# Feed-forward output projections as seven block products in place of direct ones

## The chip, the cores and the metric

The kernel runs on one core of a Trainium2 chip. The metric is the device time of one launch in microseconds; lower is better. The core has five engines with a queue each: TensorE (PE) multiplies matrices, VectorE (DVE), ScalarE (ACT) and GpSimd (POOL) work on elements, and SyncE (SP) issues most DMA transfers. Every queue is worked off strictly in its own order; engines wait for each other by semaphores.

## The reference

One decoder layer on 1024 prompt tokens and 8 single-token samples, 1032 columns in all (kept transposed: channels on partitions, tokens along the free dimension). The part that matters:

```python
D_MODEL, D_FF = 1024, 2816
def _swiglu(h, wi, wo):
    u = h @ wi                            # 1024 -> 2 * 2816
    gate, up = u[..., :D_FF], u[..., D_FF:]
    return (jax.nn.silu(gate) * up) @ wo  # 2816 -> 1024

h = _layer_norm(DN_ALPHA * h + 0.5 * _swiglu(h, ffn1_wi, ffn1_wo), g0, b0)
mix, ... = _mixer(h, ...)                 # RWKV-7 and RG-LRU branches
h = _layer_norm(DN_ALPHA * h + mix, g1, b1)
h = _layer_norm(DN_ALPHA * h + _xattn(h, ...), g2, b2)
h = _layer_norm(DN_ALPHA * h + 0.5 * _swiglu(h, ffn2_wi, ffn2_wo), g3, b3)
```

## The kernel before

Every fp32 operand of a matrix product is split into a high and a low part (ACT copies the high part, DVE subtracts: `split`, L228 and L229), and each product is three matmuls into the same psum tile (`mm3`, L125 to L127). `raw_tile` gives the staging tile into which a DMA loads what is to be split.

The function `ffn` runs twice, first (FFN1) and last (FFN2) in the program. `KT` is 8 tiles of 128 input channels, `JT` is 22 tiles of 128 hidden channels, `HN` is 258, a quarter of the 1032 columns.

The **up stage** computes hidden tiles 0 and 1 directly (`classic`) and the other 20 in ten pairs (`pair(j)`, j = 2, 4, ... 20). A pair has two halves, gate and up; a half multiplies a 2x2 block of weight by a 2x2 block of activations in seven block products instead of eight ("forms", in the order B11, B21, T1, B22, T2, T3, T4), each for two column halves p. So the stage has 20 half-pairs; the text calls them h0 to h19. `left(j)` loads four weight blocks of 128x512 per half-pair and makes four weight sums of them on POOL (L334, through `pool_tt`); the fourth of these sums is split for the form B22. DVE puts the products together into the hidden tiles `g` (`TT`, L333), and SP stores them to DRAM (`HID`, L407).

The **down stage** multiplies the 22 hidden tiles by `wo` directly: they are taken in eight groups of two or three; `loads` brings a group's tiles back from `HID`, loads its rows of `wo` and splits both; for each of 8 output tiles and 3 column chunks of 344 (`CH3`), `down_tile` sums a group in psum and DVE adds it to the accumulator `acc` (L442). POOL adds the residual `src` (L464). The last group is woven with the layer norm of the three chunks (`ln_stat_step`, `ln_finish`).

The order in which each queue gets its instructions is set by a scheduler from the program's dependencies and buffers, not by the order of the source lines.

Of the kernel before, what the change touches and what calls it, by code (L numbers as in the profile page):

```python
# [153 lines left out]
def ln_finish(S, st, li, c0, n, final=None, keep=None):  # L154

    S.pend.append((c0, c0 + n))
    return ln_stream(S, st, li, c0, n, final, keep)


def ln_stream(S, st, li, c0, n, final, keep):  # L160
# [11 lines left out]
    adds = nc.gpsimd if final is None or c0 + n < NT else nc.vector  # L172
# [49 lines left out]
LN_STEPS = 20  # L222

# [59 lines left out]
def ffn(S, octx, wi, wo, li, src, pre=(), final=None, keep=None, after=None):  # L283
# [5 lines left out]

    nc, tc = S.nc, S.tc  # L290
    HID = S.dram.tile([JT, 128, NT], F32, name="HID%d" % li)
    with ExitStack() as ctx:
# [39 lines left out]
        gt = pool(uctx, "fg", 6)  # L332
        TT = lambda o, a, b, op: nc.vector.tensor_tensor(out=o, in0=a, in1=b, op=op)  # L333
# [30 lines left out]
        def pair(j):  # L364
# [46 lines left out]
        groups = [[0, 1]] + [[3 * g + i for i in (2, 3, 4)] for g in range(5)] + [[17, 18], [19, 20, 21]]  # L411
        hd, wt = {}, {}
        S.hlseq = itertools.cycle([S.whl] * 2 + [S.hlx] * 2)

        def loads(js, to=None):
            for j in js:
                hd[j] = to() if to else (S.HH[:, j % KT, :], S.HL[:, j % KT, :])
                for p in range(2):
                    N = slice(2 * HN * p, 2 * HN * p + 2 * HN)
                    x = raw_tile(S)  # L420
                    nc.sync.dma_start(out=x, in_=HID[j, :, N])
                    split(nc, [t[:, N] for t in hd[j]], x)
                wt[j] = load_split(S, wo[128 * j:128 * j + 128, :])

        loads(groups[0])
        uctx.close()
        S.norms = Norms(S, octx, 344)
        hlast = pool(ctx, "fhl", 3)
        xw = pool(ctx, "fwo", 5)
        S.hlseq = itertools.cycle([S.hlx] * 2 + [xw] * 2 + [S.whl] * 3 + [xw] * 3 + [S.hlx] * 2)  # L430

        def down_tile(js, m, ni, st=None):
            c0, n = CH3[ni]
            q = psum(n)
# [11 lines left out]
        def down_last(js, ni, st):
            for m in range(KT):
                down_tile(js, m, ni, st)
                yield

        banks = itertools.cycle([ps])
        last = lambda: [hlast.tile([128, NT], F32R, tag="h" + x, name="h" + x) for x in "hl"]
        for g, js in enumerate(groups[:-1]):
            loads(groups[g + 1], last if g + 2 == len(groups) else None)
            for m in range(KT):
                for ni in range(3):
                    down_tile(js, m, ni)
            if 2 <= g < 6:
                for k in (2 * g - 4, 2 * g - 3):
                    for p in range(2):  # L460
                        a = S.acc[:, k, 2 * HN * p:2 * HN * p + 2 * HN]
                        x = raw_tile(S)
                        nc.sync.dma_start(out=x, in_=src[k, :, 2 * HN * p:2 * HN * p + 2 * HN])
                        nc.gpsimd.tensor_tensor(out=a, in0=a, in1=x, op=ALU.add)  # L464
        if after is not None:
            ahead(S, after)
        pre = []
        for ni in range(3):
            st = SimpleNamespace()
            weave((down_last(groups[-1], ni, st), KT), *pre)  # L470
            pre = [(ln_finish(S, st, li, *CH3[ni], final, keep), LN_STEPS)]
# [72 lines left out]
def mixer(octx, S, I, O, MG, HD, pre):  # L544
# [13 lines left out]
    with ExitStack() as ctx:  # L558
# [807 lines left out]
        return [norm(3)]  # L1366
# [49 lines left out]
def attention(S, I, li, pre, after, keep):  # L1416
# [3 lines left out]
    with ExitStack() as ctx:  # L1420
# [200 lines left out]
        return [norm(3)]  # L1621
# [121 lines left out]
```

## Time and profile before

| | us |
|---|---|
| median of three runs | 3177.53 |
| fastest, slowest of them | 3172.7, 3178.56 |
| profiled execution, its own time | 3173.59 |
| its span (first to last instruction) | 3171.8 |
| PE busy in the span | 2997.5 (95%) |
| DVE busy | 2196.4 (69%) |
| ACT busy | 1433.0 (45%) |
| POOL busy | 669.7 (21%) |
| down stage of FFN1, 459.7 to 726.4 | 266.7 |
| down stage of FFN2, 2884.5 to 3145.1 | 260.6 |

The profiled execution is 3.9 us faster than the median. Busy shares are over the whole span; the work below is done by stage, since the stages have different limits.

### The profile page before, as it was taken

The page shows a single profiled execution, that of the slowest core. Times are in us where ns is not written, and L with a number is a line of the kernel's source. Part 1 is how long each engine was busy: PE and PEld are TensorE (multiplying, and loading weights), DVE is VectorE, ACT ScalarE, POOL GpSimd, SP SyncE. Part 2 cuts the span into 40 slices and gives each one's busy share as a digit, 9 for nine tenths or more (in the row PEclk, how much of TensorE's full clock was granted, in tenths as well). Part 3 has the DMA queues.
Part 4 walks back from the last instruction along what each step waited for, and adds up shares of the span by engine and source line. Part 5 has one row for each costly group of instructions (what it writes and reads, how often), then busy time and mean ns, then how long its engine had stood idle before and what let it go on. Part 6 is the DMA issues. An engine that isn't in the chain of part 4 may idle for free. (4 is left out here: it accounts for less than half of the span.)

```text
span 3171.8 us, 63384 instructions
## 1 busy us (share of the span) xinstructions
PE 2997.5 (95%) x23324; PEld 2835.5 (89%) x23324; DVE 2196.4 (69%) x5903; ACT 1433.0 (45%) x3193; POOL 669.7 (21%) x718
## 2 busy tenths in 40 slices
PE   8999999999999999999999989889897999999997
PEld 8999999998888888888887768788897999999997
DVE  7666665564367788877787877666778666666556
ACT  5333342125465565566556655354235333334212
POOL 2222210123021121122112122350005222220111
PEclk9999999999999999999999979799998999999998
DMA  4222243413645555545554454654433222225321
GB/s 139 79 83 78 81 148 109 126 49 110 223 134 137 142 146 145 143 133 144 147 147 131 140 161 131 183 168 134 147 121 121 73 78 81 78 80 161 111 84 54
DMA packets 375943, 386.74 MB, mean 122 GB/s; under 512 B 153904, under 2 KB 267600, under 8 KB 375632
## 3 DMA queue, kind: packets, MB, share of 16 engines
q1 hardware_dynamic: 363344, 348.86, 37.3%
q0 software_dynamic: 12288, 33.83, 3.0%
q8 instruction: 183, 3.00, 0.4%
q14 instruction: 128, 1.05, 0.1%
HBM read 277.54 MB, written 105.23 MB: 121 GB/s over the span
## 5 line engine op out<-in xcount | busy, mean ns | idle before, releaser
L125 PE MATMUL ps<-HH,wh 128*128 128x258 f32 (+1 forms) x2384 | 718.7, 302 | 18.3 <-ACT HH L510 7.4
L126 PE MATMUL ps<-HL,wh 128*128 128x258 f32 (+1 forms) x2384 | 717.1, 301 | 0.6 <-POOL HL L215 0.6
L127 PE MATMUL ps<-HH,wl 128*128 128x258 f32 (+1 forms) x2384 | 715.9, 300 | 0.0
L125 PE MATMUL g<-HH,wh 128*128 128x344 f32 (+2 forms) x1840 | 618.5, 337 | 20.7 <-ACT ev L556 4.5
L127 PE MATMUL g<-HH,wl 128*128 128x344 f32 (+2 forms) x1840 | 596.1, 325 | 2.2 <-DVE wl L100 2.2
L126 PE MATMUL g<-HL,wh 128*128 128x344 f32 (+2 forms) x1840 | 594.1, 323 | 0.5 <-POOL HL L215 0.2
L125 PEld LDWEIGHTS ps<-HH,wh 128*128 128x128 f32 x2384 | 451.4, 189 | 20.7 <-ACT HH L510 7.4
L126 PEld LDWEIGHTS ps<-HL,wh 128*128 128x128 f32 x2384 | 451.2, 189 | 1.4 <-POOL HL L215 0.9
L127 PEld LDWEIGHTS ps<-HH,wl 128*128 128x128 f32 x2384 | 450.6, 189 | 0.0
L125 PEld LDWEIGHTS g<-HH,wh 128*128 128x128 f32 x1840 | 354.5, 193 | 38.1 <-ACT ev L556 6.3
L127 PEld LDWEIGHTS g<-HH,wl 128*128 128x128 f32 x1840 | 354.0, 193 | 7.4 <-DVE wl L100 3.1
L126 PEld LDWEIGHTS g<-HL,wh 128*128 128x128 f32 x1840 | 355.2, 193 | 5.5 <-POOL HL L215 1.4
L334 POOL TENSOR_TENSOR raw<-raw 128x512 f32<-128x512 f32 x160 | 213.8, 1336 | 566.0 <-DVE wl L229 359.0
L228 ACT ACTIVATE wh<-raw 128x512 fp32r<-128x512 f32 x280 | 176.5, 631 | 322.0 <-PE ps L126 260.9
L229 DVE TENSOR_TENSOR wl<-raw,wh 128x512 fp32r<-128x512 f32 x280 | 203.0, 726 | 139.0 <-ACT wh L228 132.1
L99 ACT ACTIVATE wh<-raw 128x512 fp32r<-128x512 f32 x302 | 185.1, 626 | 221.8 <-PE ps L126 77.6
L100 DVE TENSOR_TENSOR wl<-raw,wh 128x512 fp32r<-128x512 f32 x302 | 217.7, 728 | 91.8 <-ACT wh L99 89.4
L442 DVE SCALAR_TENSOR_TENSOR acc<-ps,acc 128x344 f32<-128x344 f32 x336 | 168.4, 512 | 144.2 <-PE ps L127 143.5
L644 POOL DMA_DIRECT2D GD<-ev x150 | 84.4, 563 | 632.5 <-ACT ev L556 411.8
L551 DVE TENSOR_TENSOR pr<-tq,iv 128x2 f32<-128x2 f32 (+30 forms) x496 | 159.7, 322 | 2.8
L556 ACT ACTIVATE ev<-g 128x344 f32<-128x344 f32 x192 | 86.9, 453 | 106.1 <-PE g L127 103.6
L464 POOL TENSOR_TENSOR acc<-acc,raw 128x516 f32<-128x516 f32 x32 | 42.7, 1340 | 420.0 <-DVE acc L442 322.4
(407 smaller groups left out, 6515.5 us busy)
## 6 DMA issues: line engine op xcount, KB each, us to landing
raw<-in_wi_dram SPq DMA_DIRECT2D x176, 256.0 KB
raw<-in_w_in_dram SPq DMA_DIRECT2D x116, 256.0 KB
raw<-in_wo_dram SPq DMA_DIRECT2D x104, 256.0 KB
GD<-ev POOLq DMA_DIRECT2D x150, 172.0 KB, 2.6
raw<-HID SPq DMA_DIRECT2D x88, 258.0 KB
HID<-g SPq DMA_DIRECT2D x80, 258.0 KB
tg<-GD SPq DMA_DIRECT2D x32, 512.0 KB
wt<-T SPq DMA_DIRECT2D x160, 64.0 KB
```

What stands on the lines that cost most here:

```text
L99: nc.scalar.activation(out=hi, in_=raw, func=AF.Identity)
L100: S.low.tensor_tensor(out=lo, in0=raw, in1=hi.bitcast(F32), op=ALU.subtract)
L125: nc.tensor.matmul(ps, wh, xh, start=first, stop=False)
L126: nc.tensor.matmul(ps, wh, xl, start=False, stop=False)
L127: nc.tensor.matmul(ps, wl, xh, start=False, stop=last)
L228: nc.scalar.activation(out=hi, in_=x, func=AF.Identity)
L229: nc.vector.tensor_tensor(out=lo, in0=x, in1=hi.bitcast(F32), op=ALU.subtract)
L334: pool_tt = lambda o, a, b, op: nc.gpsimd.tensor_tensor(out=o, in0=a, in1=b, op=op)
L442: nc.vector.scalar_tensor_tensor(out=a, in0=q, scalar=0.5 / ALPHA, in1=a, op0=ALU.mult, op1=ALU.add)
L551: TTo = lambda o, a, b, op: nc.vector.tensor_tensor(out=o, in0=a, in1=b, op=op)
L556: ACT = lambda o, a, f=AF.Identity, **kw: nc.scalar.activation(out=o, in_=a, func=f, **kw)
L644: (nc.gpsimd if then else nc.sync).dma_start(out=GD[p][:, gi, c0:c0 + n], in_=e)
```

## The change

It is all in `ffn` and the layer norm that follows it.

- **Up stage, `hidden(i, G)`:** after each pair POOL makes four differences of the hidden blocks (T1 to T4, in eight instructions of 128x258) and issues ten stores from its own queue into `HF`, one array per form. The four stores of SP into `HID` go away.
- **Up stage, `sums(i)`:** for each pair SP loads four blocks of `wo` (128x512) into the tiles w0 to w3, POOL makes four sums of 128x512 and issues four stores of them into `WF`. The pool `ff` has one buffer of each of these tiles. `hidden(0)` and `sums(0)` are for hidden tiles 0 and 1.
- **Down stage:** seven forms times two column halves make 14 passes. A pass sums one form over all 11 pairs of hidden tiles in four psum tiles of 258 columns (132 matmuls), then adds the four results to one or two quarters of `acc`. During the first pass of a form, the next form's activations are loaded from `HF` and split (`hid_prep`), during the second its weights (`w_prep`). The residual `src` is loaded straight into `acc`.
- **Layer norm:** four chunks of 258 columns instead of three of 344, beginning at the passes of T3 and T4, with two buffers for the running sum and a number of empty steps before a chunk's second part (`lag`); where a norm is woven with other work its step count is multiplied by four (`first_of`, also for the norms that the mixer and the attention hand on).

```diff
-            for m in range(2):
-                for p in range(2):
-                    nc.sync.dma_start(out=HID[j + m, :, 2 * HN * p:2 * HN * p + 2 * HN], in_=G[m][p])
+            hidden(j // 2, G)
+
+        def hidden(i, G):
+            T = [ft.tile([128, 2 * HN], F32, tag="t%d" % t, name="t%d" % t) for t in range(4)]
+            sub = lambda o, a, b: pool_tt(o, a, b, ALU.subtract)
+            for p in range(2):
+                (b11, b12), (b21, b22) = ((g[p][:, :HN], g[p][:, HN:]) for g in G)
+                N = slice(HN * p, HN * p + HN)
+                t1, t2, t3, t4 = (t[:, N] for t in T)
+                for f, b in ((0, b11), (1, b21), (3, b22)):
+                    nc.gpsimd.dma_start(out=HF[i, f, :, N], in_=b)
+                sub(t1, b12, b11)
+                sub(t3, b22, b12)
+                sub(t2, b22, t1)
+                sub(t4, t2, b21)
+            for f, t in zip((2, 4, 5, 6), T):
+                nc.gpsimd.dma_start(out=HF[i, f], in_=t)
+
+        def sums(i):
+            t = [ft.tile([128, 512], F32, tag="w%d" % x, name="w%d" % x) for x in range(5)]
+            for x, b in zip(t, ((0, 0), (0, 1), (1, 1), (1, 0))):
+                nc.sync.dma_start(out=x, in_=weight(i, *b))
+            yield
+            a11, a21, a22, a12, s1 = t
+            pool_tt(s1, a21, a22, ALU.add)
+            pool_tt(a21, a11, a21, ALU.subtract)
+            pool_tt(a11, a22, a21, ALU.subtract)
+            pool_tt(a12, a12, a11, ALU.subtract)
+            for n, x in enumerate((s1, a11, a21, a12)):
+                nc.gpsimd.dma_start(out=WF[i, n], in_=x)
+            yield
 
         for j in range(2, JT, 2):
+            w = sums(j // 2)
+            next(w)
             pair(j)
...
+        def one_pass(f, p, st=None):
...
+            qs = [psum(HN) for _ in range(4)]
+            for k in range(NJ):
+                if f < 6:
+                    (w_prep if p else hid_prep)(f + 1, k)
+                for m in range(4):
+                    step(m, k, qs[m])
+                yield
+            for m in range(4):
+                result(m, qs[m])
...
+        for k in range(KT):
+            nc.sync.dma_start(out=S.acc[:, k, :], in_=src[k])
+        pre = []
+        for f, p in itertools.product(range(7), range(2)):
+            st = SimpleNamespace() if f > 4 else None
+            weave((one_pass(f, p, st), NJ), *pre)
...
```

What the scheduler makes of it shows in the queues. First POOL's queue in the up stage of FFN1, where `raw` are weight blocks of the up stage. Before, a half-pair's four sums follow each other and nothing lies between them; these two groups of four are those of h4 and h5:

```order
L334 TENSOR_TENSOR raw_1760<-raw_1756,raw_1758 128x512
L334 TENSOR_TENSOR raw_1756<-raw_1752,raw_1756 128x512
L334 TENSOR_TENSOR raw_1752<-raw_1760,raw_1752 128x512
L334 TENSOR_TENSOR raw_1754<-raw_1754,raw_1752 128x512
L334 TENSOR_TENSOR raw_2019<-raw_2015,raw_2017 128x512
L334 TENSOR_TENSOR raw_2015<-raw_2011,raw_2015 128x512
L334 TENSOR_TENSOR raw_2011<-raw_2019,raw_2011 128x512
L334 TENSOR_TENSOR raw_2013<-raw_2013,raw_2011 128x512
```

After, the same place has this (w0 to w4 are the tiles of `sums`, `g` a hidden tile; the first two rows and the last but one are h4's first three sums):

```order
L345 TENSOR_TENSOR raw_1844<-raw_1840,raw_1842 128x512
L345 TENSOR_TENSOR raw_1840<-raw_1836,raw_1840 128x512
L345 TENSOR_TENSOR w4_4133<-w1_4130,w2_4131 128x512
L451 DMA WF0_133<-w4_4133 128x512
L345 TENSOR_TENSOR w1_4130<-w0_4129,w1_4130 128x512
L345 TENSOR_TENSOR w0_4129<-w2_4131,w1_4130 128x512
L451 DMA WF0_133<-w1_4130 128x512
L345 TENSOR_TENSOR w3_4132<-w3_4132,w0_4129 128x512
L451 DMA WF0_133<-w0_4129 128x512
L451 DMA WF0_133<-w3_4132 128x512
L345 TENSOR_TENSOR raw_1836<-raw_1844,raw_1836 128x512
L427 DMA HF0_132<-g_1263 128x258
```

The scheduler puts all 11 groups of `sums` of an up stage ahead of the weight sums of h7, in FFN1 as in FFN2. Between the first weight sum of h1 and the fourth of h6 POOL's queue of FFN1 now holds 23 weight sums of the up stage, 44 of `sums`, 16 differences of `hidden` and 66 stores; before it held the 23 alone. In FFN2, counted from the third weight sum of h1, there are 21, 44, 16 and 66.

SP's queue at the loads for h4 and h5, before (`in_wi1_dram` is the up weight, `HID` takes the stores of the hidden tiles):

```order
L341 DMA raw_1752<-in_wi1_dram 128x512
L341 DMA raw_1756<-in_wi1_dram 128x512
L341 DMA raw_1758<-in_wi1_dram 128x512
L341 DMA raw_2011<-in_wi1_dram 128x512
L341 DMA raw_2013<-in_wi1_dram 128x512
L341 DMA raw_2015<-in_wi1_dram 128x512
L341 DMA raw_2017<-in_wi1_dram 128x512
L407 DMA HID0_131<-g_1214 128x516
```

And after, for h6 (its four `raw` blocks are 2405 to 2411):

```order
L443 DMA w2_4717<-in_wo1_dram 128x512
L352 DMA raw_2099<-in_wi1_dram 128x512
L443 DMA w1_4716<-in_wo1_dram 128x512
L352 DMA raw_2101<-in_wi1_dram 128x512
L443 DMA w0_4715<-in_wo1_dram 128x512
L443 DMA w3_4718<-in_wo1_dram 128x512
L352 DMA raw_2405<-in_wi1_dram 128x512
L443 DMA w2_5286<-in_wo1_dram 128x512
L352 DMA raw_2407<-in_wi1_dram 128x512
L443 DMA w0_5284<-in_wo1_dram 128x512
L443 DMA w1_5285<-in_wo1_dram 128x512
L443 DMA w3_5287<-in_wo1_dram 128x512
```

Loads of `sums` that wait for one buffer now stand ahead of and between the loads of the up weights.

PE's queue where the down stage begins, before:

```order
L127 MATMUL ps_6000<-T4h_148,wl_5981 128x258
L125 MATMUL ps_6142<-HH_79,wh_6030 128x344
L126 MATMUL ps_6142<-HL_80,wh_6030 128x344
L127 MATMUL ps_6142<-HH_79,wl_6031 128x344
L125 MATMUL ps_6142<-HH_79,wh_6050 128x344
L126 MATMUL ps_6142<-HL_80,wh_6050 128x344
L127 MATMUL ps_6142<-HH_79,wl_6051 128x344
```

And after:

```order
L127 MATMUL ps_6376<-T4h_150,wl_6357 128x258
L125 MATMUL ps_6571<-HH_79,wh_6428 128x258
L126 MATMUL ps_6571<-HL_80,wh_6428 128x258
L127 MATMUL ps_6571<-HH_79,wl_6429 128x258
L125 MATMUL ps_6572<-HH_79,wh_6428 128x258
L126 MATMUL ps_6572<-HL_80,wh_6428 128x258
L127 MATMUL ps_6572<-HH_79,wl_6429 128x258
```

Up to the first of these rows PE's queue is the same before and after; from there three matmuls of 344 columns per step become three of 258, and four psum tiles are filled in turn.

## Rows read from the trace of the kernel before

**Rows 1.** Busy time of each engine in stretches, (x) counts instructions.

```profile
core 0: us, PE busy (x) PEld busy (x) DVE busy (x) ACT busy (x) POOL busy (x), PEclk, DMA share, GB/s
70.00:450.00 380.00, 380.00 (x3170) 380.00 (x3169) 255.30 (x474) 140.96 (x291) 94.67 (x72) 1.00 0.26 81
500.00:650.00 150.00, 150.00 (x953) 150.00 (x952) 84.12 (x152) 27.31 (x46) 16.02 (x12) 1.00 0.34 103
459.70:726.40 266.70, 261.80 (x1644) 259.08 (x1642) 161.41 (x328) 71.16 (x138) 42.63 (x39) 0.99 0.33 101
2884.50:3145.10 260.60, 257.59 (x1640) 255.79 (x1639) 155.43 (x292) 62.66 (x120) 32.80 (x29) 1.00 0.31 96
```

**Rows 2.** The same view, two stretches inside the mixer and the attention.

```profile
800.00:850.00 50.00, 50.00 (x328) 42.75 (x328) 16.51 (x42) 22.64 (x48) 0.00 (x0) 1.00 0.68 233
2400.00:2450.00 50.00, 35.48 (x208) 33.17 (x209) 39.26 (x90) 30.64 (x79) 29.82 (x36) 0.81 0.34 108
```

**Rows 3.** Timeline (start us, duration us, operation): DVE and PE, end of the program.

```profile
3144.84 1.16 DVE L442 SCALAR_TENSOR_TENSOR acc<-ps,acc 128x344 f32<-128x344 f32 x2
...
3145.12 0.32 PE L127 MATMUL ps<-hh,wl 128*128 128x344 f32 x1
...
3167.61 0.57 DVE L205 SCALAR_TENSOR_TENSOR acc<-acc,lng,ln 128x344 f32<-128x344 f32 x1
```

**Rows 4.** Timeline of POOL: weight sums of h1 and h6 in FFN1, h1 in FFN2.

```profile
61.33 6.61 POOL L334 TENSOR_TENSOR raw<-raw 128x512 f32<-128x512 f32 x4 [7.82 <-DVE wl L229]
...
165.08 1.29 POOL L334 TENSOR_TENSOR raw<-raw 128x512 f32<-128x512 f32 x1 [1.86 <-issue]
...
2485.95 1.30 POOL L334 TENSOR_TENSOR raw<-raw 128x512 f32<-128x512 f32 x1 [0.93 <-DVE wl L229]
...
2500.50 2.65 POOL L334 TENSOR_TENSOR raw<-raw 128x512 f32<-128x512 f32 x2 [10.43 <-DVE wl L229]
```

**Rows 5.** Groups by line, POOL: count, busy us, mean ns, idle before.

```profile
L334 POOL TENSOR_TENSOR raw<-raw 128x512 f32<-128x512 f32 x160 | 213.8, 1336 | 566.0 <-DVE wl L229 359.0 <-DMA raw<-in_wi_dram 101.7 <-issue 56.2
L644 POOL DMA_DIRECT2D GD<-ev x150 | 84.4, 563 | 632.5 <-ACT ev L556 411.8 <-DMA za<-GD 100.5 <-ACT BK L556 30.7
```

**Rows 6.** Timeline of PE: first matmul of h6 in FFN1 and FFN2.

```profile
177.58 0.28 PE L125 MATMUL ps<-HH,wh 128*128 128x258 f32 x1
...
2602.37 0.28 PE L125 MATMUL ps<-HH,wh 128*128 128x258 f32 x1
```

**Rows 7.** Groups by line and form, ACT and DVE, 56.6 to 460 us.

```profile
L228 ACT ACTIVATE wh<-raw 128x512 fp32r<-128x512 f32 x137 | 86.4, 631 | 157.6 <-PE ps L126 127.9 <-issue 17.9 <-DVE wl L229 6.6
...
L229 DVE TENSOR_TENSOR wl<-raw,wh 128x512 fp32r<-128x512 f32 x137 | 98.7, 722 | 66.8 <-ACT wh L228 63.5
L333 DVE TENSOR_TENSOR g<-g,c 128x258 f32<-128x258 f32 x77 | 50.3, 663 | 1.6
L333 DVE TENSOR_TENSOR g<-u,p 128x258 f32<-128x258 f32 x40 | 23.2, 580 | 1.4
L333 DVE TENSOR_TENSOR c<-u,p 128x258 f32<-128x258 f32 x39 | 19.9, 510 | 1.0
L333 DVE TENSOR_TENSOR p<-p,ps 128x258 f32<-128x258 f32 x40 | 16.9, 424 | 23.2 <-PE ps L127 20.6
```

**Rows 8.** The tile FD: 24 stores of POOL's queue, 128x344, until they landed.

```profile
DMA to landing us min/median/max: 2.1/2.4/5.1
```

**Rows 9.** Timelines of DVE and POOL where both read two SBUF tiles.

```profile
112.37 0.69 DVE L229 TENSOR_TENSOR wl<-raw,wh 128x512 fp32r<-128x512 f32 x1
...
113.53 2.96 POOL L334 TENSOR_TENSOR raw<-raw 128x512 f32<-128x512 f32 x2 [7.90 <-DVE u L333]
...
115.26 1.78 DVE L229 TENSOR_TENSOR wl<-raw,wh 128x512 fp32r<-128x512 f32 x1
...
38.80 0.74 POOL L246 TENSOR_TENSOR acc<-acc 128x258 f32<-128x258 f32 x1
```

More of the change, by code (lines that the diff above doesn't have):

```diff
@@ L222, with first_of @@
 LN_STEPS = 20
+def first_of(norm):
+    return norm[0], 4 * norm[1]
 def split(nc, to, x):
@@ L446, in down_last @@
[L446 to L471, printed above, removed]
+            next(w)
+            if j == 8:
+                G = [[gt.tile([128, 2 * HN], F32, tag="g%d" % m, name="g", bufs=3) for _ in range(2)] for m in range(2)]
+                for m, p in itertools.product(range(2), range(2)):
+                    nc.sync.dma_start(out=G[m][p], in_=HID[m, :, 2 * HN * p:2 * HN * p + 2 * HN])
+                hidden(0, G)
@@ new lines, in ffn, with hid_prep @@
+            if j == 14:
+                for _ in sums(0):
+                    pass
+        FORMS = ("B11", "B21", "T1", "B22", "T2", "T3", "T4")
+        room = SimpleNamespace()
+        HX, W = {}, {}
+        def hid_prep(f, k):
+            x = raw_tile(S)
+            nc.sync.dma_start(out=x, in_=HF[k, f])
+            c = f % 2
+            if k < KT:
+                to = [t[:, k, :].rearrange("q (p c n) -> q c p n", p=2, c=2)[:, c] for t in (S.HH, S.HL)]
+            else:
+                to = [t[:, k - KT] for t in room.hx[c]]
+            split(nc, to, x.rearrange("q (p n) -> q p n", p=2))
+            HX[f, k] = to
@@ new lines, in ffn @@
+        for k in range(KT):
+            hid_prep(0, k)
+            if k < 7:
+                w_prep(0, k)
+        uctx.close()
+        S.norms = Norms(S, octx, 2)
+        hx = pool(ctx, "fhx", 1)
+        room.hx = [[hx.tile([128, NJ - KT, 2, HN], F32R, name="hx%d%s" % (c, y)) for y in "hl"] for c in range(2)]
+        room.u = pool(ctx, "fu", 1).tile([128, 4, 2 * HN], F32, name="fu")
+        xw = pool(ctx, "fwo", 6)
+        S.hlseq = itertools.cycle([xw] * 6 + [S.hlx] * 4 + [S.whl] * 3)
@@ new lines, in ffn @@
+        for k in range(7, NJ):
+            if k >= KT:
+                hid_prep(0, k)
+            w_prep(0, k)
+        banks = itertools.cycle([ps])
+        for k in range(KT):
+            nc.sync.dma_start(out=S.acc[:, k, :], in_=src[k])
[3 more added lines that the diff above has]
+            weave((one_pass(f, p, st), NJ), *pre)
+            if (f, p) == (6, 0) and after is not None:
+                ahead(S, after)
+            if st is not None:
+                pre = [first_of((ln_finish(S, st, li, 2 * HN * p + HN * (6 - f), HN, final, keep, 8 if (f, p) == (6, 1) else 28),
+                                 LN_STEPS))]
@@ L1365, in mixer @@
         ahead(S, I["wq"][0])
-        return [norm(3)]
+        return [first_of(norm(3))]
 NCA = [(0, 256), (256, 256), (512, 256), (768, 264)]
@@ L1620, in attention @@
             weave((attend(h), 44 if h < 3 else 50), (samples(h), 21), (fill(h), 49 if h < 3 else 40))
-        return [norm(3)]
+        return [first_of(norm(3))]
 @with_exitstack
```

104 lines of the change are left out of this document (67 added, 37 removed).

## The prediction

> **What bounds the kernel now.** I read the stage windows first, because busy shares over the whole span mix stages with different limits. In both stages of the feed-forward PE has no gap to speak of [rows 1]: 380 of 380 us in the up stage, 261.8 of 266.7 and 257.6 of 260.6 in the two down stages, with the clock at its upper level, 2.4 GHz (granted 0.99 to 1.00). So time there is matmuls times pitch. In the up stage 3170 matmuls of 258 columns take 380 us, 0.1199 us each; in the down stage 953 of 344 columns take 150 us, 0.1574 us each [rows 1]. A form of a half-pair is 2 halves x 4 blocks x 3 = 24 matmuls, 2.88 us; a half-pair is 168 matmuls, 20.15 us. POOL works 94.7 of 380 us there and DVE 255.3 [rows 1]: neither sets the end, and POOL is where the change puts its work. What I then looked for is when POOL's results are due.
>
> **What is removed on PE.** A down stage has 8 x 3 x 22 x 3 = 1584 matmuls of 344 columns: 249.3 us. Afterwards 7 forms x 2 halves x 4 x 11 x 3 = 1848 of 258: 221.6 us. Gain 27.7 us per feed-forward, **55.4 us** together. That is the whole gain; the up stage's own matmuls stay as they are.
>
> **What the down stage gives back.**
> - At each of 13 borders between passes, PE has two of six psum tiles free (0.72 us for two steps of 3), then needs one that has just been emptied. DVE empties 344 columns in 0.58 us [rows 3] and 258 in 0.42 [rows 7]; T1 and T2 need two operations per result. I take 3 us per feed-forward for it, **6 us** together (bounds 0 and 13 x 0.6 = 8 per feed-forward).
> - Splits: per pass 11 of 0.63 on ACT and 0.72 on DVE [rows 7], 6.9 and 7.9 us in a pass of 15.8: hidden by the matmuls. Loads: 11 x 264 KB per 15.8 us is 184 GB/s, below the 233 GB/s that a stretch moved at 0.68 of the DMA engines' time [rows 2]. Hidden too, except at the start, where `src` (4.2 MB) must reach `acc` behind the last stores and in the same queue as the next form's activations: 10 MB within about 45 us, 222 GB/s. I take 1 us per feed-forward, **2 us** (bounds 0 and 11: what the first two passes' 10 MB need at 233 GB/s, 43 us, less 31.6).
> - One more norm chunk, against a shorter last one: the end from the last matmul to the last DVE operation is 23 us with 344 columns [rows 3] and goes by serial steps, not columns alone. I take **3 us** more (bounds -3 and +8). `first_of` starts norms sooner where they are woven: 2 us less, from 0 to 4.
>
> Sum of the down stage: 55.4 - 6 - 2 - 3 + 2 = **46 us gained**.
>
> **What the up stage loses: POOL's queue.** `hidden` adds 8 operations and 10 stores per pair, `sums` 4 and 4. Spread evenly that is harmless: per pair of 40.3 us POOL would have 8 + 4 operations of 1.34, 8 of 0.78 and 14 stores of 0.56 [rows 5], 30 us. But the queue isn't even: the scheduler puts all 11 `sums` ahead of h7. Take FFN1, from the first weight sum of h1, at 61.33 [rows 4], whose loads are ahead of the new ones, to the fourth of h6.
> - 67 operations of 128x512. The mean is 1.336 us [rows 5], two back to back took 2.65 [rows 4]; I take 1.37 with the gap: 91.8 us.
> - 16 of 128x258: one took 0.74 [rows 9]; with a gap like that of the longer ones 0.78: 12.5 us.
> - 66 stores: 0.563 us in the mean [rows 5]: 37.0 us.
>
> Together 141.3 us, so the fourth sum of h6 starts at 202.6 at the earliest; it started at 165.08 before [rows 4]. When is it due? Its split feeds B22, the fourth form of h6. h6 starts on PE at 177.58 [rows 6], B22 8.64 later, at 186.2; before that 1.29 for the sum, 0.63 and 0.72 for the split [rows 4, 7]. Due at 183.6: POOL is **19.0 us late**. In FFN2 there are 65 + 16 + 66 from the third sum of h1, at 2485.95 [rows 4]: 138.5 us, 2624.5, due 6.0 after 2602.37 [rows 6]: **16.1 us late**. The smallest prices without gaps (1.29 for a sum [rows 4], 0.74, 0.56) leave 13 and 10.
>
> Two things make POOL later still.
> - Waits of `sums` on itself. w0 to w4 have one buffer; SP's load of the next group's w1 waits until the store of this one has landed, and POOL waits for the load. A store of POOL's landed after 2.4 us in the median [rows 8]; for SP's loads of 256 KB no row has a landing, and I bound it by 2 to 3 us, about that store. After the store of w1 POOL has one sum and two stores left (2.5 us), plus what the queue puts between the groups. Over ten borders that leaves 8 us (load 2.0) to 16 us (load 3.0). I take **10 us** per feed-forward.
> - DVE. Where both engines read two SBUF tiles, they hold each other up: a split of 0.69 us took 1.78 beside two POOL sums, which took 2.96 instead of 2.65 [rows 4, 9]. DVE's operations with two SBUF inputs are 137 of 0.72, 77 of 0.66, 40 of 0.58 and 39 of 0.51 in 403 us [rows 7]: 192 us, or 88 operations and 57 us in the 120 us from POOL's start to h6; at the split's undisturbed 0.69 [rows 9] and the 0.42 of the same operation with a psum input [rows 7], 48 us. POOL's own price per sum holds some of it already, and in a third of its time here it issues stores, which need no tile reads of this kind. Between 0 and 48 us I take **8 us** per feed-forward.
>
> The Trainium skill, "GPSIMD Engine Reference", section 1 (Specifications), says that GpSimd's SBUF interfaces are shared with VectorE and contended by instructions with two SBUF inputs; the disturbed pair agrees. Read as full exclusion, each of the 48 us would go on top of POOL's 141, and the sum would come out 40 us per feed-forward higher than mine. Its section 4.1 (Engine selection) tells to keep two-input elementwise work off GpSimd as about twice as slow; here 1.34 against 0.72 us [rows 5, 7], and no run yet shows the 20 operations per pair elsewhere.
>
> What waits: PE at h6's B22 or, since half-pairs before it are pushed as well, in smaller pieces from h3 on; SP's loads for h5 and h6 stand behind loads that wait for POOL, so also B11 may be late. The sum of the pieces is POOL's lateness, 19.0 + 10 + 8 = 37 and 16.1 + 10 + 8 = 34 us. With gaps PE's clock may be granted less (0.81 in a stretch with PE busy 35 of 50 [rows 2]): 2 us, from 0 to 10. **Loss 73 us.** After h7 POOL needs some 23 us of the 40 per pair and catches up; nothing more is lost there.
>
> **Sum.** 3173.6 - 46 + 73 = 3200.6 on the profiled execution's basis; the median stands 3.9 above it, so **3204 us**.
>
> **The rivals.**
> 1. *POOL's lateness stays near its floor* (the other side, faster). If loads for `sums` land fast enough and DVE fits into POOL's stores, 8 to 20 us are lost per feed-forward; with 46 to 55 gained that is 3138 to 3172, middle 3155. It decides at 23 us of lateness per feed-forward. For it: half of the DVE work reads psum (0.42, undisturbed); POOL's smallest prices give 13 and 10. Against: the 16 + 19 us are counted instructions at the mean price, and the single-buffered tiles can't be free of waits. Chance 0.30.
> 2. *Full exclusion*: each two-input DVE operation delays POOL, and load waits are 16 us: 19 + 48 + 16 = 83 and 80, less 46, so +117: 3294; half-way to my forecast 3249. DVE then is late as well, 88 operations waiting up to 1.3 us each in a stretch where it is two thirds busy. For it: 1.78 against 0.69. Against: the mean of 1.336 beside the same DVE work. Chance 0.15.
> 3. *No measurable difference* (within 0.2%, about what a measurement of this kernel can tell, 6.4 us): lateness 20 to 26. Chance 0.08.
> 4. My forecast, 3184 to 3245: 0.47.
>
> Faster 0.30, same 0.08, slower 0.62. The range for 8 in 10 takes in the upper part of rival 1 and the lower of rival 2: **3155 to 3250**; the forecast's own is 3184 to 3245.
>
> **What would show it.** Right: in the profile after, PE has gaps between about 100 and 200 us and again between 2530 and 2640, ended by DVE's or ACT's split behind POOL's L345; POOL is near full there, with the fourth sum of h6 about 37 us behind 165; the stages from h7 on run at 20.15 us per half-pair; the down stages take 225 to 235 us. Wrong: if PE stays full through h6, or if POOL idles there on loads for more than 20 us, or if the down passes show PE idle for more than 1 us per border, waiting for DMA.

## The result and the profile after

The changed kernel took **3275.88 us** in the median (3269.64 to 3277.39, 4 runs) against 3178.05 us of the kernel before in the same comparison: 3.1% slower, ratio 1.0305 with a 95% interval of 1.0285 to 1.0326. The prediction had the sign and the place, not the size: it said 3204 us, with 3155 to 3250 as its range. The profiled execution has a span of 3267.9 us, 96.1 more than before.

First the four feed-forward stages, up 1, up 2, down 1 and down 2, in the view of stretches (columns as in [rows 1]), and three pieces inside up 1 (h1 with the end of h0, h4, h7):

```profile
56.10:524.10 468.00, 417.33 (x3360) 413.76 (x3359) 324.99 (x510) 142.02 (x316) 301.35 (x348) 0.95 0.45 146
2532.70:2995.90 463.20, 418.70 (x3361) 415.24 (x3360) 327.99 (x502) 139.95 (x308) 300.50 (x348) 0.95 0.45 146
524.10:779.40 255.30, 240.14 (x1938) 235.80 (x1937) 163.28 (x317) 113.66 (x219) 58.16 (x77) 0.98 0.55 175
2995.90:3248.10 252.20, 239.55 (x1938) 235.43 (x1937) 157.43 (x290) 105.41 (x191) 43.56 (x58) 0.99 0.55 175
...
61.30:96.20 34.90, 34.90 (x293) 34.90 (x292) 18.79 (x30) 9.83 (x23) 26.15 (x25) 1.00 0.63 206
159.90:196.50 36.60, 22.80 (x171) 21.87 (x170) 21.99 (x27) 5.91 (x13) 27.26 (x32) 0.81 0.50 166
256.40:276.60 20.20, 20.20 (x171) 20.20 (x170) 17.55 (x34) 8.31 (x19) 9.20 (x11) 1.00 0.39 116
```

PE stood still or ran slowly in the up stages, which before had no gap [rows 1]. One half-pair, h4 (159.90 to 196.50), took 36.6 us in place of 20.15, with a mean granted clock of 0.81; h7 took its old time again, h8 and h9 were late once more (22.1 and 24.0 us), and from h10 on nothing is lost. The account, from the first matmuls of stages and half-pairs in PE's timelines of both kernels:

| stretch | after less before, us |
|---|---|
| up 1, to the start of h7 | +59.4 |
| up 1, h7 to its end | +5.7 |
| down 1, to the mixer's first matmul | -13.3 |
| mixer and attention, to h1 of FFN2 | +0.2 |
| up 2 | +60.2 |
| down 2, to the last matmul of the output projection | -8.6 |
| from there to the end | -6.9 |

(PE reached h1 of FFN1 0.5 us earlier than before.) The up stages lose 125 us where 73 were forecast, and the down stages with their tail give back 29 where 46 were forecast. A down stage takes 255.3 and 252.2 us, not the 225 to 235 that the prediction expected to see.

What POOL did from h1 to the fourth weight sum of h6 is in the groups of that stretch, 61 to 233 us, which answer to [rows 5]; the first row is the view of stretches, the last one is DVE's split:

```profile
61.00:233.00 172.00, 128.60 (x993) 126.13 (x992) 92.80 (x130) 36.26 (x83) 135.28 (x149) 0.88 0.58 191
L345 POOL TENSOR_TENSOR w<-w,w 128x512 f32<-128x512 f32 x44 | 59.6, 1355 | 33.8 <-DMA w<-in_wo_dram 30.9 <-issue 1.8
L345 POOL TENSOR_TENSOR raw<-raw 128x512 f32<-128x512 f32 x23 | 30.6, 1331 | 8.6 <-DMA raw<-in_wi_dram 8.0
L451 POOL DMA_DIRECT2D WF<-w x44 | 24.4, 556 | 2.1 <-POOL w L345 1.8 <-DMA w<-in_wo_dram 0.3
L345 POOL TENSOR_TENSOR t<-g 128x258 f32<-128x258 f32 x8 | 5.8, 730 | 0.1
...
L234 DVE TENSOR_TENSOR wl<-raw,wh 128x512 fp32r<-128x512 f32 x38 | 48.3, 1282 | 65.3 <-ACT wh L233 65.2
```

The counts are those of the prediction (44 and 23), and so are the prices: 1.355 and 1.331 us a sum, 0.556 a store, 0.730 a difference. What is new is the idle time: POOL waits 36.7 of the 172 us, 31 of them for a block of `wo` to land. DVE's split takes 1.28 us in place of 0.72, but DVE is idle for 65 us in front of these splits, so that little of the time can go there.

How POOL's lateness reaches PE is in the timeline at h2, engine by engine (POOL, ACT, DVE, PE):

```profile
104.45 1.26 POOL L345 TENSOR_TENSOR w<-w,w 128x512 f32<-128x512 f32 x1 [1.78 <-DMA w<-in_wo_dram]
105.67 1.26 POOL L345 TENSOR_TENSOR raw<-raw 128x512 f32<-128x512 f32 x1
...
106.96 2.19 ACT L233 ACTIVATE wh<-raw 128x512 fp32r<-128x512 f32 x4 [16.72 <-POOL raw L345]
...
107.62 1.66 DVE L234 TENSOR_TENSOR wl<-raw,wh 128x512 fp32r<-128x512 f32 x1 [15.74 <-ACT wh L233]
109.21 0.41 DVE L344 TENSOR_TENSOR u<-p,ps 128x258 f32<-128x258 f32 x1
...
109.67 0.58 PE L125 MATMUL ps<-HH,wh 128*128 128x258 f32 x1 [10.18 <-DVE u L344]
```

The sum at 105.67 is h2's fourth, for the form B22. ACT waits 16.7 us for it and DVE 15.7 us for ACT, at the head of their queues. Behind that split in DVE's queue stands `u<-p,ps`, which empties a psum tile of h1's form T2. PE has filled its eight psum tiles (T2, T3 and T4 of h1, B11 of h2, two each) and stops after B11 of h2, two forms ahead of the one that needs the late weights. The split itself takes 1.66 us here, against 0.69 undisturbed [rows 9]: 1 us of PE's 10.2.

What h8 and h9 lose (5.7 us, and 6.9 in FFN2) has the same source, POOL catching up. DVE's and ACT's timelines there show a wait for a hidden tile that POOL has not read yet, and one for a late sum:

```profile
293.48 0.42 DVE L344 TENSOR_TENSOR g<-p,ps 128x258 f32<-128x258 f32 x1 [7.58 <-POOL t L345]
...
302.17 0.63 ACT L233 ACTIVATE wh<-raw 128x512 fp32r<-128x512 f32 x1 [6.74 <-POOL raw L345]
```

### The profile page after: what moved, and what is told of

Same layout as the page of the kernel before. It is cut to its first block, busy times and chain, and to the rows that moved or that the text cites. A ratio compares the mean times of both kernels' runs of the same rounds, so it can differ in the third digit from the quotient of the medians.

```text
span 3267.9 us, 65856 instructions
## 1 busy us (share of the span) xinstructions
PE 2983.1 (91%) x23910; PEld 2811.7 (86%) x23910; DVE 2302.8 (70%) x5875; ACT 1486.7 (45%) x3333; POOL 1092.0 (33%) x1326
## 5 line engine op out<-in xcount | busy, mean ns | idle before, releaser
L125 PE MATMUL ps<-HH,wh 128*128 128x258 f32 (+1 forms) x2368 | 698.3, 295 | 114.6 <-DVE u L344 84.0
L126 PE MATMUL ps<-HL,wh 128*128 128x258 f32 (+1 forms) x2368 | 690.2, 291 | 0.1
L127 PE MATMUL ps<-HH,wl 128*128 128x258 f32 (+1 forms) x2368 | 688.8, 291 | 0.2 <-DVE wl L234 0.2
L234 DVE TENSOR_TENSOR wl<-raw,wh 128x512 fp32r<-128x512 f32 x434 | 421.1, 983 | 260.2 <-ACT wh L233 258.4
L125 PEld LDWEIGHTS ps<-HH,wh 128*128 128x128 f32 x2368 | 461.8, 195 | 124.6 <-DVE u L344 88.5
L233 ACT ACTIVATE wh<-raw 128x512 fp32r<-128x512 f32 x434 | 268.6, 626 | 530.3 <-PE ps L126 252.8
L126 PEld LDWEIGHTS ps<-HL,wh 128*128 128x128 f32 x2368 | 461.5, 195 | 0.8 <-DVE HL L621 0.5
L100 DVE TENSOR_TENSOR wl<-raw,wh 128x512 fp32r<-128x512 f32 x214 | 155.5, 733 | 80.5 <-ACT wh L99 77.5
L99 ACT ACTIVATE wh<-raw 128x512 fp32r<-128x512 f32 x214 | 132.5, 625 | 89.1 <-PE g L126 20.1
L385 ACT ACTIVATE g<-g 128x258 f32<-128x258 f32 x160 | 66.3, 415 | 234.1 <-DVE g L344 232.8
L345 POOL TENSOR_TENSOR acc<-acc,fu 128x258 f32<-128x258 f32 x48 | 38.5, 820 | 337.4 <-DVE fu L498 282.0
L345 POOL TENSOR_TENSOR w<-w,w 128x512 f32<-128x512 f32 x88 | 119.4, 1357 | 65.2 <-DMA w<-in_wo_dram 57.7
```

Of the source, the lines that this page charges most:

```text
L99: nc.scalar.activation(out=hi, in_=raw, func=AF.Identity)
L100: S.low.tensor_tensor(out=lo, in0=raw, in1=hi.bitcast(F32), op=ALU.subtract)
L125: nc.tensor.matmul(ps, wh, xh, start=first, stop=False)
L126: nc.tensor.matmul(ps, wh, xl, start=False, stop=False)
L127: nc.tensor.matmul(ps, wl, xh, start=False, stop=last)
L233: nc.scalar.activation(out=hi, in_=x, func=AF.Identity)
```

## The experiments

Ten kernels were run. Two theories stood against each other at the start. **Q**: strict queues, with 11 groups of `sums` bunched in front of the up stage's weight sums and waiting for their one set of buffers. **X**: POOL and DVE exclude each other whenever both read two SBUF tiles, so that POOL's element work costs time wherever it stands. A diff is against the changed kernel unless the text says otherwise, and `...` marks lines left out. "Up loss" below is how much later h19's end is against h1's start than before, in FFN1 and FFN2, from PE's timelines; in the changed kernel it is 65 and 60 us.

### Without the weight sums

```diff
-            w = sums(j // 2)
-            next(w)
             pair(j)
-            next(w)
...
-            if j == 14:
-                for _ in sums(0):
-                    pass
...
-            src = (weight(k, 0, 0), weight(k, 1, 0), WF[k, 0], WF[k, 3], WF[k, 1], WF[k, 2], weight(k, 1, 1))[f]
+            src = (weight(k, 0, 0), weight(k, 1, 0), weight(k, 0, 1), weight(k, 1, 1), weight(k, 0, 1), weight(k, 1, 0), weight(k, 1, 1))[f]
```

> The weight sums are left out (no loads, sums and stores of them in the up stage; the down stage loads plain weight blocks in their place, so its products are not those of the reference); the differences and stores of the hidden tiles stay on GpSimd. Theory Q (GpSimd's strict queue: 44 sums ahead of the up stage's own weight sums, each group waiting about 3 us for its one set of buffers): most of the 125 us that the two up stages lost come back, 3276 - 115 = 3160. Rival X (GpSimd and VectorE exclude each other whenever both read two SBUF tiles, so time is lost in proportion to GpSimd's work): hidden's 88 differences per feed-forward (69 us) stay and the 44 sums (60 us) go, about half comes back, 3215.

Measured: 3168.45 us, ratio to before 0.9959 (0.9944 to 0.9974). Up loss 1.1 and 1.6 us, although all of `hidden` is still on POOL. The sums, with their loads and stores, are nearly the whole loss of the up stage, and X is off by 47 us. The down stages give back less here (7.7 us in FFN1), which is why the total isn't lower.

### One group of sums per pair

```diff
-            t = [ft.tile([128, 512], F32, tag="w%d" % x, name="w%d" % x) for x in range(5)]
+            t = [ft.tile([128, 2 * HN], F32, tag="t%d" % x, name="w%d" % x)[:, :512] for x in range(4)]
+            t.append(ft.tile([128, 512], F32, tag="w4", name="w4"))
```

> All the work of the changed kernel, but the weight sums use the tiles of the hidden differences (t0 to t3), so that a group of sums can't start before the hidden tiles of the pair before it are stored: one group per pair in GpSimd's queue. Theory Q: GpSimd needs some 30 us of the 40 of a pair and is never far behind, so up to 10 us are lost per feed-forward: 3155 to 3180. Rival X: the same work on the same two engines, so the loss stays, 3250 or more. Rival D (the DMA engines, 0.6 busy in the slow stretch, deliver the up weights late): the same bytes, spread, about half of the loss stays, 3210.

Measured: 3202.3 us, ratio 1.0063 (1.0041 to 1.0085). Up loss 14.5 and 15.0 us: three quarters of it came back with the same work. The total missed Q's interval, among other things since the down stage of FFN1 gave back 1.2 us only (13.3 in the changed kernel). It lies near rival D's 3210, but D had half of the loss staying in the up stages, and a quarter stayed; a later run (two sets of buffers) speaks against D more directly. The rest of the up loss is again POOL's queue: in its timeline a group of `sums` waits 6 us for its loads, and the next sums for an up weight stand behind that group; ACT waits 14.1 us for one of them and DVE 12.9 us for ACT.

```profile
375.38 1.28 POOL L345 TENSOR_TENSOR w<-w,w 128x512 f32<-128x512 f32 x1 [6.02 <-DMA w<-in_wo_dram]
...
383.33 4.31 POOL L345 TENSOR_TENSOR raw<-raw 128x512 f32<-128x512 f32 x3
...
384.63 0.63 ACT L233 ACTIVATE wh<-raw 128x512 fp32r<-128x512 f32 x1 [14.10 <-POOL raw L345]
...
385.30 1.20 DVE L234 TENSOR_TENSOR wl<-raw,wh 128x512 fp32r<-128x512 f32 x1 [12.91 <-ACT wh L233]
```

### The up stage's weight sums on VectorE

All four `pool_tt` of `left` become `TT`.

```diff
-            pool_tt(s1, a21, a22, ALU.add)
+            TT(s1, a21, a22, ALU.add)
```

> The up stage's own weight sums (160 in both feed-forwards) are made by VectorE in place of GpSimd; the weight sums of the down stage stay bunched on GpSimd. Theory Q: TensorE no longer depends on GpSimd's queue and keeps going; VectorE gets 4 more operations of 0.7 us per half-pair (13.5 to 16.3 of 20.15 us): 3150 to 3185. Rival X: VectorE is held up by GpSimd's bunched sums and has more to do itself: 3260 or more.

Measured: 3266.95 us, ratio 1.0268 (1.0237 to 1.0298); up loss 51 and 51. The time lies in X's interval; Q as I had put it expected TensorE to be free of POOL, and that failed. But what holds DVE is not POOL's arithmetic. SP's and DVE's timelines:

```profile
95.27 13.32 SPq L443 DMA_DIRECT2D w<-in_wo_dram  x5
108.68 0.38 SPq L352 DMA_DIRECT2D raw<-in_wi_dram  x1
...
119.27 3.17 DVE L344 TENSOR_TENSOR raw<-raw 128x512 f32<-128x512 f32 x1 [17.63 <-DMA raw<-in_wi_dram]
```

SP stands for 13 us at loads of `sums`, whose buffers wait for POOL's sums and for POOL's stores to land, and the up weights (`in_wi`) are behind them. DVE then waits 17.6 us for a weight block. So there is a second way from the bunch to PE, SP's queue.

### The same, with the loads of sums on GpSimd's queue

This line besides the edit of the run before:

```diff
-                nc.sync.dma_start(out=x, in_=weight(i, *b))
+                nc.gpsimd.dma_start(out=x, in_=weight(i, *b))
```

> The up stage's weight sums on VectorE, as in the run that took 3267, and the loads of the down stage's weight blocks issued from GpSimd's queue in place of SyncE's. If SyncE's queue is what stopped TensorE there (its loads for sums wait for a store of GpSimd's to land, and the up weights stand behind them), TensorE now waits for neither queue: up stages lose under 10 us each, 3155 to 3185. Rival X (GpSimd's sums hold VectorE up): GpSimd's element work is the same, 3240 or more.

Measured: 3253.27 us, ratio 1.0232 (1.0213 to 1.0251); up loss 44 and 40. Neither of the two ways is left, and still most of the loss is. DVE's timeline names a third:

```profile
120.82 0.42 DVE L344 TENSOR_TENSOR g<-p,ps 128x258 f32<-128x258 f32 x1 [13.34 <-POOL t L345]
...
182.29 0.42 DVE L344 TENSOR_TENSOR g<-p,ps 128x258 f32<-128x258 f32 x1 [20.59 <-POOL t L345]
```

DVE waits for a hidden tile `g` (three buffers), which is free when `hidden` has read it, and `hidden` stands behind `sums` in POOL's queue. The expectation counted as X's what is again POOL's order. No run took this third way away by itself; it is read from the trace.

### Only the loads of sums on GpSimd's queue

The line just shown on the changed kernel itself, with the up stage's weight sums on POOL.

> The changed kernel, with only the loads of sums moved from SyncE's queue to GpSimd's; the up stage's weight sums stay on GpSimd. If GpSimd's lateness alone decides, 44 more issues of 0.56 us and a round trip that is now wholly in its queue make it worse than the changed kernel: 3280 to 3340. If SyncE's blocked queue is what decides there too, most of the loss goes: 3200 or less.

Measured: 3311.0 us, ratio 1.0409 (1.039 to 1.0429); up loss 79 and 71. Here POOL's lateness is enough by itself: freeing SP's queue didn't help, and with 44 issues more on POOL the loss grew by 14 and 10 us.

### Two sets of buffers for the sums

```diff
-            t = [ft.tile([128, 512], F32, tag="w%d" % x, name="w%d" % x) for x in range(5)]
+            t = [ft.tile([128, 512], F32, tag="w%d" % x, name="w%d" % x, bufs=2) for x in range(4)]
...
-            a11, a21, a22, a12, s1 = t
-            pool_tt(s1, a21, a22, ALU.add)
+            a11, a21, a22, a12 = t
             pool_tt(a21, a11, a21, ALU.subtract)
-            pool_tt(a11, a22, a21, ALU.subtract)
-            pool_tt(a12, a12, a11, ALU.subtract)
-            for n, x in enumerate((s1, a11, a21, a12)):
+            pool_tt(a22, a22, a21, ALU.subtract)
+            pool_tt(a12, a12, a22, ALU.subtract)
+            pool_tt(a11, a11, a22, ALU.add)
+            for n, x in enumerate((a11, a22, a21, a12)):
```

(The room comes from the pool `ftmp`, closed after `classics`.)

> The changed kernel with two sets of the weight-sum tiles (the sums are made in place in four tiles, which needs no fifth; the same four sums up to rounding); the bunch of 11 groups stays, and the stores stay on GpSimd. Theory Q: of GpSimd's 32 us of waits for those tiles per feed-forward most go, its 135 us of work stay, so each up stage loses about 40 us in place of 63: 3205 to 3240. Rival W (the waits are all of it): 3165 or less. Rival X (GpSimd against VectorE): the same element work, 3265 or more.

Measured: 3248.11 us, ratio 1.0213 (1.0185 to 1.024); up loss 40.6 and 39.3, as Q had it. POOL's groups, 61 to 199 us, ahead of them the view of that stretch:

```profile
61.00:199.00 138.00, 112.68 (x817) 109.18 (x816) 107.29 (x112) 30.57 (x72) 131.68 (x144) 0.90 0.70 233
L347 POOL TENSOR_TENSOR w<-w,w 128x512 f32<-128x512 f32 x44 | 59.6, 1365 | 1.2 <-DMA w<-in_wo_dram 0.3
L347 POOL TENSOR_TENSOR raw<-raw 128x512 f32<-128x512 f32 x20 | 27.8, 1391 | 10.1 <-DVE wl L234 7.9 <-DMA raw<-in_wi_dram 1.2 <-POOL raw L347 0.7
```

The 31 us of waits are down to 0.3, and the up loss falls by 24.5 and 20.9 us; the other 40 fit the bunch's work, which stayed. The stretch also speaks against rival D: the DMA engines are busier than in the changed kernel's bunch (0.70 against 0.58) while less is lost, so busy DMA engines are not what sets the loss. The total missed its interval by 8 us, mainly because less came back behind the up stages than in the changed kernel: -11.6 in place of -13.3 to the mixer, and mixer and attention took 10.3 us more than before where the changed kernel had +0.2.

### All stores on SyncE's queue

```diff
-                    nc.gpsimd.dma_start(out=HF[i, f, :, N], in_=b)
+                    nc.sync.dma_start(out=HF[i, f, :, N], in_=b)
...
-                nc.gpsimd.dma_start(out=HF[i, f], in_=t)
+                nc.sync.dma_start(out=HF[i, f], in_=t)
...
-                nc.gpsimd.dma_start(out=WF[i, n], in_=x)
+                nc.sync.dma_start(out=WF[i, n], in_=x)
```

> All stores of hidden and sums issued from SyncE's queue in place of GpSimd's. Theory Q: GpSimd is rid of 66 issues of 0.56 us, 37 us, in the bunched stretch, but SyncE's queue now waits for GpSimd's results ahead of its loads, and the buffers' round trip stays: the up stages lose 30 to 60 us each in place of 63, 3210 to 3270. Were the issues the main thing (rival S), all 37 us per feed-forward would come back: 3200 or less.

Measured: 3211.59 us, ratio 1.0094 (1.0064 to 1.0124); up loss 34.1 and 30.3. It is at the lower end of Q's interval, and 31 and 30 us came back, of the 37 that rival S had for all the issues. The part of the change that put the stores on GpSimd's queue costs half of what the up stages lose.

### Paced sums and stores on SyncE

The two edits of those runs together: the tiles of `sums` are those of `hidden`, and the three store lines say `nc.sync`.

> All the work of the changed kernel: one group of weight sums per pair (they use the tiles of the hidden differences) and all stores of hidden and sums from SyncE's queue. Theory Q (two strict queues, GpSimd's and SyncE's, with bunched sums and one set of buffers): the run with stores on SyncE took 3212 with 64 us lost in its up stages; without the bunch nearly all of it comes back, 3147 to 3160. Rival X (GpSimd and VectorE exclude each other): the element work is the same, 3195 or more.

Measured: **3168.5 us**, ratio 0.9961 (0.9947 to 0.9976): 0.4% below the kernel before, with all of the changed kernel's work. Up 1, up 2, down 1, down 2:

```profile
56.60:466.20 409.60, 404.83 (x3361) 403.44 (x3360) 314.27 (x499) 141.23 (x313) 238.59 (x200) 1.00 0.51 164
2486.30:2891.60 405.30, 403.84 (x3363) 403.36 (x3362) 308.41 (x491) 140.49 (x307) 241.53 (x200) 1.00 0.51 165
466.20:724.40 258.20, 242.74 (x1937) 237.86 (x1935) 168.24 (x328) 116.13 (x222) 57.28 (x72) 0.97 0.56 177
2891.60:3146.10 254.50, 239.26 (x1936) 234.29 (x1935) 159.72 (x301) 105.96 (x193) 41.57 (x51) 0.99 0.56 177
```

Up loss 6.6 and 2.1 us, with the same 88 differences and 44 sums per feed-forward on POOL: X is out as the cause of the loss. The time missed its interval by 8.5 us: the down stages gave back only 10.4 and 6.2 us, and mixer and attention took 9 us more than before.

### The same with two buffers of the shared tiles

Against the run before:

```diff
-            T = [ft.tile([128, 2 * HN], F32, tag="t%d" % t, name="t%d" % t) for t in range(4)]
+            T = [ft.tile([128, 2 * HN], F32, tag="t%d" % t, name="t%d" % t, bufs=2) for t in range(4)]
...
-            t = [ft.tile([128, 2 * HN], F32, tag="t%d" % x, name="w%d" % x)[:, :512] for x in range(4)]
+            t = [ft.tile([128, 2 * HN], F32, tag="t%d" % x, name="w%d" % x, bufs=2)[:, :512] for x in range(4)]
```

> As the run with paced sums and stores on SyncE, with two buffers of each tile that hidden and sums share. If waits for these tiles still cost something there, this is 5 to 15 us faster; if not, within 5 us of it.

Measured: 3175.33 us, ratio 0.9988 (0.9974 to 1.0001); up loss 6.0 and 6.9. It is 6.8 us slower than the run before, outside both intervals, so a second buffer brings nothing here; since it also lets `sums` run a group further ahead, the run doesn't tell what the waits alone cost. In its profile mixer and attention took 13 us more than in the kernel before, against 9 in the run before this one, and FFN2's up loss is 4.8 us higher; why is not shown.

### The residual loaded in quarters

Against the run with paced sums and stores on SyncE:

```diff
-        for k in range(KT):
-            nc.sync.dma_start(out=S.acc[:, k, :], in_=src[k])
+        def rest(r, c):
+            for m, p in itertools.product(range(4), range(2)):
+                N = slice(2 * HN * p + HN * c, 2 * HN * p + HN * c + HN)
+                nc.sync.dma_start(out=S.acc[:, 4 * r + m, N], in_=src[4 * r + m, :, N])
...
+        rest(0, 0)
...
+            for q in {(0, 1): ((0, 1),), (1, 0): ((1, 1),), (2, 1): ((1, 0),)}.get((f, p), ()):
+                rest(*q)
```

> Paced sums and stores on SyncE (3168.5), with the residual loaded into the accumulator in quarters, each before the form that first adds to it, in place of all 4.2 MB at the first pass. If the DMA engines, 0.9 busy in the first two passes, hold TensorE there (6 us of gaps and a lower clock per feed-forward), 8 to 14 us less: 3155 to 3161. If those gaps have another cause, within 3 us of 3168.

Measured: 3167.87 us, ratio 0.996 (0.9944 to 0.9975): no gain over 3168.5. The edit made little difference to the DMA engines, so it hardly tests them: in the first two passes they were 0.85 and 0.93 busy, against 0.88 and 0.92 in the run it is compared with.

```profile
466.20:500.00 33.80, 27.74 (x207) 27.11 (x206) 23.95 (x37) 13.38 (x26) 11.22 (x12) 0.90 0.85 262
```

PE's and ACT's timelines at the first border show how PE is held there:

```profile
490.22 0.58 PE L125 MATMUL ps<-HH,wh 128*128 128x258 f32 x1 [5.51 <-ACT fu L502]
...
487.78 0.63 ACT L233 ACTIVATE HH<-raw 128x516 fp32r<-128x516 f32 x1 [4.98 <-DMA raw<-HF]
```

PE waits for `fu`, ACT's copy that empties a psum tile of the first form; ACT stood 5 us at a split whose load hadn't landed, and the copy is behind it. It is the pattern of h2 again, with a DMA in POOL's place. That bytes alone don't explain the gap shows in the run with all stores on SyncE and the sums bunched: the DMA engines were as busy in that stretch (0.94) and PE lost next to nothing.

```profile
493.70:527.00 33.30, 32.94 (x271) 32.44 (x269) 18.46 (x27) 14.68 (x26) 8.02 (x10) 1.00 0.94 321
```

## Why the prediction was right in its sign and wrong in its size

**Right: the place and the cause.** Nearly all of PE's lost time lies in h2 to h6 (59.4 of 65.1 us in FFN1), in both feed-forwards, behind the bunch of `sums` in POOL's queue; without sums the up loss is 1 to 2 us, and with the same sums paced and the stores on SP 2 to 7. POOL's counted work held too: forecast 141.3 us from h1's first to h6's fourth weight sum, measured 135.3 busy in 61 to 233 us. The size failed in several terms, first of all in POOL's waits. The prediction named a sign for that ("if POOL idles there on loads for more than 20 us"), and it came true.

**Wrong: "waits of `sums` on itself ... I take 10 us".** They were 30.9 us in FFN1's stretch. I bounded SP's load by 2 to 3 us and let it start when the store of w1 had landed, 2.4 us after its issue. In the timeline (SP, then POOL) the group's load of w1, the second of the first row, goes out only at the end of 4.1 us, when that store has landed (3.9 us after its issue), and POOL's next sum starts another 4.8 us later:

```profile
71.01 4.12 SPq L443 DMA_DIRECT2D w<-in_wo_dram  x2
75.64 0.33 SPq L352 DMA_DIRECT2D raw<-in_wi_dram  x1
76.40 3.40 SPq L443 DMA_DIRECT2D w<-in_wo_dram  x2
...
70.91 0.56 POOL L451 DMA_DIRECT2D WF<-w  x1
...
79.95 1.30 POOL L345 TENSOR_TENSOR w<-w,w 128x512 f32<-128x512 f32 x1 [4.86 <-DMA w<-in_wo_dram]
```

POOL's group began at 79.95, 8.5 us after its store of w1 had been issued (70.91 to 71.47), where the prediction had 2.4 + 2 to 3. With two sets 24.5 and 20.9 us came back: the bound of 16 was too low. With that the lateness at h6's fourth sum adds up in FFN1: forecast 37 us; 6 less for the work (135.3 in place of 141.3), 27 more for all waits (36.7 in place of 10), 8 less for contention, which the work holds already: 50, and 49.6 was measured.

**Wrong: "its split feeds B22 ... due at 183.6".** I took the matmul that uses the weights as the deadline. PE stops 5.8 us (two forms) earlier, when a psum tile isn't emptied because the emptying stands behind the split in DVE's and ACT's queues. At h6 itself PE's and POOL's timelines have (the last row is the view of that half-pair):

```profile
227.49 0.28 PE L125 MATMUL ps<-HH,wh 128*128 128x258 f32 x1
...
236.28 0.58 PE L125 MATMUL ps<-HH,wh 128*128 128x258 f32 x1 [5.76 <-DVE u L344]
...
233.23 1.27 POOL L345 TENSOR_TENSOR raw<-raw 128x512 f32<-128x512 f32 x1
...
227.30:256.40 29.10, 22.75 (x170) 22.05 (x170) 19.13 (x29) 6.33 (x14) 23.43 (x30) 0.88 0.46 147
```

PE starts h6 at 227.5, stops after B11 and goes on at 236.3, 1.8 us after the fourth sum. POOL's start at 233.2 is 49.6 after the due time I gave, and PE was 58.9 behind at h7: the 9 us between are these 5.8 and, as far as I can see, the lower clock of that half-pair (granted 0.88 from 227.3 to 256.4, PE busy 22.75 us in place of 20.15).

**Wrong: "nothing more is lost there" after h7, and 2 us for the clock.** POOL's catching up cost another 5.7 and 6.9 us in h8 and h9, by the waits shown above. PE was busy 417.3 and 418.7 us in the up stages for the matmuls that took 403.1 before, 14 and 16 us more at the lower granted clock, where the prediction had 2 (0 to 10) for both. How much of that adds to the time, and how much stands where PE would else have waited for POOL, no run here separates.

**Wrong: the bound on SP's side.** That "SP's loads ... may be late" was named, but counted within POOL's lateness. The run with the weight sums on VectorE shows that it stops PE by itself, and the next run shows a third way over the buffers of `g`, which I hadn't seen. POOL's lateness was enough by itself as well (only the loads moved: +14 and +10).

**Not needed: 8 us for DVE's contention.** POOL's sums cost 1.33 to 1.36 us in the stretch, against 1.336 before. It is DVE that takes most of the delay (1.28 against 0.72 us a split), while it has time. The Trainium skill, "GPSIMD Engine Reference", section 1 (Specifications), says that GpSimd's SBUF interfaces are shared with VectorE and contended by VectorE's instructions with two SBUF inputs; the rows agree. The second rival got the time nearly right (+117, measured +96), by luck. Operation by operation its exclusion is in the trace: of the splits in 61 to 233 us, 13 begin while a POOL sum runs, and each of them ends 0.55 to 0.63 us after that sum does, as in [rows 9] (115.26 + 1.78 against 113.53 + 2.96). But the price that it put on POOL's queue, 48 us, isn't there: the 28 sums that begin while a DVE operation with two SBUF inputs runs take 1.42 us in the mean, the 30 that run beside none 1.28, which is about 4 us over all sums of the stretch. And had the exclusion set the time, the paced runs would be slow.

**Wrong: 46 us gained in the down stages; 29 measured, tail included.** The matmuls are as counted. Four terms were off. The borders, 3 us per feed-forward, and the first passes, 1 us: PE's idle time in a down stage is 15.2 and 12.7 us, of which 4.9 and 3.0 were there before [rows 1], so 10 us each were given back in place of 4. In FFN1 about 3 of the 10 are PE's waits for the norm, not at borders. The rows at two borders and at the longest wait for the norm:

```profile
563.50 0.58 PE L125 MATMUL ps<-HH,wh 128*128 128x258 f32 x1 [3.01 <-ACT fu L501]
...
695.93 0.39 PE L125 MATMUL ps<-HH,wh 128*128 128x258 f32 x1 [1.55 <-DVE fu L498]
...
742.49 0.77 PE L169 MATMUL ln<-lns,ones_d 128*128 128x258 f32 x1 [3.50 <-DVE lns L145]
```

The clock, which I had not put into the down stages: after the first passes' gaps it is granted at 0.84 for a stretch (558 to 580 us), and 1848 x 0.1199 = 221.6 plus the norms' 14.1 is 235.7 against 240.1 busy. Before, the same sum is 249.3 + 9.6 = 258.9 against 261.8, so that 1.5 of these 4.4 us are new. And the norm chunk: I looked at the end of the program, where the time went the other way (-6.9 in place of +3), and missed that one chunk more lies inside the stage. The norm's psum tile `ln`, before (down 1) and after (down 1), PE busy in the second number:

```profile
459.70:726.50 266.80, 9.58 (x58) 7.71 (x58) 12.23 (x26) 0.00 (x0) 0.99 0.33 101
```

```profile
524.10:779.40 255.30, 14.08 (x87) 11.04 (x87) 17.52 (x48) 0.00 (x0) 0.98 0.55 175
```

That is 4.5 us more in FFN1, and with it its down stage adds up: 27.7 less for the matmuls, 10.3 more idle, 1.5 for the clock and 4.5 for the norm make 11.4 less, as the stretches have it (266.7 to 255.3).

**Left open:** why the paced kernels gain so much less in the down stages (1 to 12 us in FFN1) than the one with the bunch and stores on SP (18.8); the copy behind waiting splits is seen at the first border, but no run took it away, and the run with the residual in quarters left the DMA engines as busy as before.

## What to carry to other kernels

A strict queue makes work urgent that isn't: side work with no deadline, placed by a scheduler wherever its inputs allow, delays everything behind it, so pace it with a resource of the main loop (here a shared tile, worth 45 to 51 us in each of the two stages). The due time of an operand isn't the instruction that reads it: look for what stands behind the wait in the queues of all engines that touch it, the emptying of psum above all. A single set of buffers over store and reload is a round trip through two queues; price it as store landing, plus each issue, plus load landing, for the tiles that the next group reads first (here 8.5 us).

## What was not expected of the hardware

The same stretch of the mixer took different times, at different granted clocks, in kernels that do the same work there. The mixer's PE stretch between two equal DVE operations took 33.6 us in the kernel before and 40.1 in the changed one, at 0.95 and 0.79 granted, with a like gap of PE of 2.8 us near its start in both; with stores on SP it took 34.0 at 0.95. Before, then after:

```profile
1007.00:1041.00 34.00, 30.92 (x269) 27.81 (x270) 19.78 (x60) 19.08 (x45) 6.27 (x9) 0.95 0.50 134
```

```profile
1057.00:1097.00 40.00, 35.96 (x265) 32.39 (x266) 19.56 (x56) 18.85 (x43) 5.88 (x8) 0.79 0.43 116
```

That is 6.5 us more in one stretch, 5.0 of them PE's busy time at the lower clock (35.96 against 30.92). In the kernels here, mixer and attention together took 0 to 13 us more than before, about as much as the best version gains; among the changed kernels only the feed-forwards differ, and in the stretches other than this one the cause was not followed.
